# Four more attention weights split ahead of time, a narrower first query tile, and one block order swapped, in a two-layer decoder trunk

## The chip, the cores and the metric

The kernel runs on one core of a Trainium2 chip. The core has a matrix engine (TensorE: PE for the matrix products, PEld for the loads of the stationary operand that go with them), three engines for element-wise work (VectorE: DVE, ScalarE: ACT, GpSimd: POOL) and a queue engine (SyncE: SP) that issues the DMA transfers here. The metric is the time of one execution on the device in microseconds (us). Engines run side by side, each in its own fixed order of instructions, and wait for one another through semaphores.

## What is computed

Input `x` has 512 tokens of 1024 channels. The reference, cut to what matters here:

```python
for layer in range(2):
    h = rms_norm(x, mix_pre_g[layer])
    if layer == 0:
        m = pool_mixer(h, pool_w[0], pool_scale[0])          # causal averages, then 4 maps of 256x256
    else:
        q = h @ w_q                                          # 16 heads of 64
        o = stick_breaking_attention(q, k, v)                # key s < query t
        m = o @ w_o
    x = x + rms_norm(m, mix_post_g[layer])
    h = rms_norm(x, mlp_pre_g[layer])
    x = x + rms_norm(square(relu(h @ w_up[layer])) @ w_down[layer], mlp_post_g[layer])
    if layer == 0:
        k, v = split(rms_norm(x, kv_norm_g) @ w_kv)
```

In the attention, with `z = q k^T / 8`, a query's weight on key `s` is `sigmoid(z)` times the product of `1 - sigmoid(z)` over the keys between `s` and the query. Everything is float32.

## The kernel before

**Numbers in two parts.** A product in float32 is done as three products of a cheaper float32 form. Each operand is split into a high part (a rounding copy on ACT) and a low part (the difference, a subtraction on DVE); then high*high, high*low and low*high are added up in PSUM (`mm3`, and `up_block` for weights of which 128 columns stand in the array). A weight block of 128x1024 (512 KB) therefore costs a load, one ACT copy and one DVE subtraction before PE can use it. `weight` does this where the block is needed: it loads into a tile `raw`, copies the high part (L128) and subtracts the low part (L130).

**Weights kept in DRAM.** The layer-0 MLP also splits blocks for the attention in advance. `split_apart`, called once for each of the products of that MLP that `steps` lists, is a pipeline of four steps per block: load it into a free tile (`apart`, `spare` or `grow`); in the next call scale it on ACT if it carries a norm's gain (L139); in the next split it (L191 on ACT into `wx`, L192 on DVE back into its own tile); in the next store both parts to a DRAM tile `kept` (L172). Thirty blocks go this way: the value blocks `v`, the key and query blocks `k` and `q`, output blocks `o` 4 to 7, and two `up` blocks of the second MLP. When `make` later comes to such a block it issues two DMAs from `kept` (L202) and no engine has to split anything. Output blocks `o` 0 to 3 are not among the thirty and go through `weight`.

**Buffers.** Split weights live in three tiles tagged `w` and one tagged `wx`; up to four blocks are made ahead (`queue`, `made`, `ahead`). A load into such a tile waits until PE has finished with the block that was in it. `wx` is used by `split_apart` during the first MLP.

**The stages.** (1) Pooling mixer of layer 0, its order written out by hand (`MIX_ORDER`), with the first halves of four `up` blocks. (2) MLP of layer 0: 32 `up` blocks (`up_block`, 24 matmuls each) and, for 28 of them, the down projection as a Strassen-like scheme of seven products for each of five groups (`Seven`, L507; operands `a` and `w` are split by L242 on ACT and L243 on DVE, differences are built by POOL L462 and DVE L481). The last four blocks of the down projection, `dn`, are plain `mm3` (`contract`); their split tiles reuse buffers of the MLP, two of them the `apart` buffers. (3) Attention. (4) MLP of layer 1, as (2) without `split_apart`.

**The attention's order** is the table `ATT_ORDER`: V = `values` (value blocks of four heads, by key tile), K and P = projections of keys and queries of a pair of heads, S = `weights` (scores, sigmoids on ACT, the running product as a scan on DVE, L867, and one multiplication, L871), T = `transposed` (PE transposes, L885, split by L242 and L243), A = `mix_pair` (weights times values, L895), O and E = `out_proj` (output projection, `mm3`, by token tiles). So `V33` is the block of values 3 for key tile 3, and `O101` is the output projection with output blocks 2 and 3 for token tiles 0 and 1. The program text sets dependences and buffers; a scheduler then orders each engine's instructions by priority and estimated times, except where `manual_schedule` fixes an order.

Of the kernel before, what the change touches and what calls it, by code (L numbers as in the profile page):

```python
# [15 lines left out]
P = 128  # L16
# [36 lines left out]
ATT_ORDER = [  # L53
    (w[0], int(w[1]), [int(c) for c in w[2:]])
    for w in """V001 K0 V02 P0 V03 S0 P1 T0 V101 S1 A0 P2 T1 V123 A1 S2 P3 T2 O00123 A2 S3 P4 V201 T3 A3
    S4 P5 T4 V223 S5 A4 P6 V301 T5 S6 A5 P7 V32 T6 S7 O101 V33 A6 T7 A7 O12 O13 E2""".split()
]


# [6 lines left out]
def trunk(ctx, tc, x, consts, gcol, grow, pw, wup, wdn, wq, wk, wv, wo, out):  # L66
# [46 lines left out]
    behind, latest = {}, {}  # L113
# [29 lines left out]
    gate, queue, made, ahead, dn_pool, att_pool = [False], [], {}, 4, [None], [None]  # L143
# [21 lines left out]
    apart, kept, going = [], {}, []  # L165

    def split_apart(mp):
        if going and going[0][1] == 3:
            k, _, raw, hi, _ = going.pop(0)
            kept[k] = dram.tile([2, P, D], F32, tag=f"kept{len(kept)}", name=name("kept"))  # L170
            for n, t in enumerate((hi.bitcast(F32), raw)):
                latest["sp"] = nc.sync.dma_start(kept[k][n], t)  # L172
        if apart:
            k, src, scaled = apart.pop(0)
            n = len(apart) % 5
            if n < 3:
                raw = mp.tile([P, D], F32, tag="apart", bufs=3, name=name("apart"))
            else:
                raw = spare_tile() if n == 3 else work.tile([P, D], F32, tag="grow", name=name("apart"))

            with tc.issue_after(latest["sp"].ins) if "sp" in latest else nullcontext():
                nc.sync.dma_start(raw, src)
            going.append([k, 0, raw, None, scaled])
        for x in going:
            k, n, raw, hi, scaled = x
            if n == 1:
                if scaled is not None:
                    scaled(raw)
            elif n == 2:
                hi = x[3] = apart_hi[0][:, len(kept) % 2]  # L190
                nc.scalar.copy(hi, raw)  # L191
                nc.vector.tensor_tensor(out=raw, in0=raw, in1=hi.bitcast(F32), op=ALU.subtract)  # L192
            x[1] += 1
# [24 lines left out]
    for l in range(2):  # L218
        if l == 1:
            n = len(queue)  # L220
            for what, i, part in ATT_ORDER:
                if what == "V" and 0 in part:
                    for h in range(2):
                        want(("v", i, h), wv[i, h], gains(C_KV * KC + 4 * h, 4))
                elif what == "P":
                    want(("k", i), wk[i], gains(C_KV * KC, KC))
                    want(("q", i), wq[i], gains(C_MIX_PRE1 * KC, KC))
                elif what == "O" and 0 in part or what == "E":
                    for c in range(2 * i, 2 * i + (2 if what == "O" else 4)):
                        want(("o", c), wo[c])  # L230
            apart.extend(x for x in queue[n:] if x[0] not in [("o", c) for c in range(4)])
            apart.extend((("up", 1, j), wup[1, j], None) for j in range(2))

            queue[n - GRP : n + GRP] = queue[n : n + GRP] + queue[n - GRP : n]
        for j in range(NJ):
            want(("up", l, j), wup[l, j])
        for j in range(NJ - GRP, NJ):
            want(("dn", l, j), wdn[l, j])
# [279 lines left out]
    def mlp(l, mp, update):  # L518
# [4 lines left out]
        plain = 2 * sum(GROUPS)  # L523
        groups = [Seven(l, firsts[g], n, mp) for g, n in enumerate(GROUPS)]

        steps = [n for n in range(1, 34)] if l == 0 else []
        squares = []
        written = {None}

        def up(j, pu=None):  # L530
            if pu is None:
                pu = ps()
                up_block(pu, get(("up", l, j)), slice(0, S))
            if j < plain:
                g = max(g for g, f in enumerate(firsts) if f <= j)
                r = groups[g].part(j - firsts[g])
            else:
                r = mp.tile([P, S], F32, tag="rp", name=name("rp"))
            nc.scalar.activation(r, pu, ACT.Relu)
            nc.scalar.activation(r, r, ACT.Square)  # L540
            if j >= plain:
                if j < plain + 3:
                    if j == plain:
                        squares.append(mp.tile([P, 3, 2, S], F32R, tag="r", bufs=2, name=name("sq")))
                    a = squares[0][:, j - plain]
                else:
                    a = work.tile([P, 2, S], F32R, tag="spare", name=name("sq"))
                split(r, a[:, 0], a[:, 1])
                squares.append((a[:, 0], a[:, 1]))
            fill()  # L550
# [18 lines left out]
        for j, (pu, w) in enumerate(first):  # L569
            up_block(pu, w, slice(S // 2, S))  # L570
            up(j, pu)
        with tc.issue_after(latest["act"].ins), tc.issue_after(latest["dve"].ins):
            for i in range(2):
                groups[0].make(i)
        for g, group in enumerate(groups):
# [10 lines left out]
            for i in range(7):  # L586
# [12 lines left out]
                else:  # L599
# [4 lines left out]
                    elif i == 5:  # L604
                        piece = lambda tag, k, bufs=1: mp.tile([P, k, D], F32R, tag=tag, bufs=bufs, name=name("dn"))
                        w, e, x = piece("w1", 3), piece("e", 1), piece("w", 3, 2)
                        c, d = (piece("apart", 1, 3)[:, 0] for _ in range(2))
# [143 lines left out]
    with tc.tile_pool(name="att", bufs=1, reuse_waits="tile") as ap:  # L751
# [79 lines left out]
        for lo, n in SEG.values():  # L831
            c = min(n - P, 1)
# [9 lines left out]
        def weights(qk, a):  # L842

            q, k, kl, u = qk[0][a], qk[1][a], kls[a], us[a]
            w = ap.tile([P, NSEG], F32, tag="w", bufs=2, name=name("w"))
            for tiles, at in (((3,), 0), ((2,), 512), ((1, 0), 896)):
                pz = ps()
                o = 0  # L850
                for i in tiles:
                    n = max(256, (i + 1) * P)
                    nc.tensor.matmul(pz[:, o : o + n], q[:, TS[i]], k[:, :n], start=True, stop=False)  # L853
                    nc.tensor.matmul(  # L854
                        pz[:, o : o + n], q[:, TS[i]], kl[:, :n], start=False, stop=True
                    )
                    o += n
                o = 0
                for i in tiles:
                    n = SEG[i][1]  # L860
                    nc.scalar.activation(  # L861
                        u[:, at + o + 1 : at + o + n], pz[:, o + 1 : o + n], ACT.Sigmoid, scale=-0.125
                    )
                    o += n
                nc.scalar.activation(w[:, at : at + o], pz[:, :o], ACT.Sigmoid, scale=0.125)
            e = ap.tile([P, NSEG], F32, tag="e", name=name("e"))
            nc.vector.tensor_tensor_scan(  # L867
                out=e[:, ::-1], data0=u[:, 1:][:, ::-1], data1=begin[:, ::-1],
                initial=0.0, op0=ALU.mult, op1=ALU.max,
            )  # L870
            nc.vector.tensor_tensor(out=w, in0=w, in1=e, op=ALU.mult)  # L871
            return w
# [134 lines left out]
```

## Time and profile before

| | |
|---|---|
| three runs | 980.87, 982.71, 986.82 us; median 982.71 us |
| profiled execution | span 984.6 us from first to last instruction |
| PE | busy 959.1 us (97%), 4804 matmuls |
| PEld | 812.2 us (82%) |
| DVE | 715.6 us (73%) |
| ACT | 566.9 us (58%) |
| POOL | 138.5 us (14%) |
| DMA | 156.88 MB, 44.4% of the 16 engines' span |
| granted PE clock, mean | 0.990 |

The profiled execution's time is known only as its span; no time of its own around the span was recorded. The span lies 1.9 us above the median of the three runs and inside their range. In the profile a busy share of PE is not a measure of speed: matmuls overlap, and each is shown as longer than the distance to the next one. A full-rate matmul of 512 columns shows 0.39 us but the next starts 0.227 us later. What a wait costs is read from starts.

### The profile page before, as it was taken

The page shows a single profiled execution, that of the slowest core. Times are in us where ns is not written, and L with a number is a line of the kernel's source. Part 1 is how long each engine was busy: PE and PEld are TensorE (multiplying, and loading weights), DVE is VectorE, ACT ScalarE, POOL GpSimd, SP SyncE. Part 2 cuts the span into 40 slices and gives each one's busy share as a digit, 9 for nine tenths or more (in the row PEclk, how much of TensorE's full clock was granted, in tenths as well). Part 3 has the DMA queues.
Part 4 walks back from the last instruction along what each step waited for, and adds up shares of the span by engine and source line. Part 5 has one row for each costly group of instructions (what it writes and reads, how often), then busy time and mean ns, then how long its engine had stood idle before and what let it go on. Part 6 is the DMA issues. An engine that isn't in the chain of part 4 may idle for free.

```text
span 984.6 us, 12507 instructions
## 1 busy us (share of the span) xinstructions
PE 959.1 (97%) x4804; PEld 812.2 (82%) x4804; DVE 715.6 (73%) x772; ACT 566.9 (58%) x979; POOL 138.5 (14%) x107
## 2 busy tenths in 40 slices
PE   9799999999999999999999999989999999999997
PEld 6688888878788788999799987888888888888885
DVE  3647589897897986376667688775487785957856
ACT  4537888978695556465556573446454444444532
POOL 1102030130402204100000000302031210302103
PEclk9899999999999999999999999989999999999999
DMA  6153777959678690242352423243333314133012
GB/s 249 44 192 98 265 275 227 416 199 346 243 277 326 232 342 3 89 169 86 129 214 89 168 108 121 77 145 108 128 102 112 128 56 181 29 127 122 22 43 87
DMA packets 43550, 156.88 MB, mean 159 GB/s; under 512 B 4449, under 2 KB 4833, under 8 KB 43490
## 3 DMA queue, kind: packets, MB, share of 16 engines
q1 hardware_dynamic: 43490, 156.07, 44.4%
q8 instruction: 38, 0.62, 0.2%
q14 instruction: 22, 0.18, 0.1%
HBM read 122.50 MB, written 33.55 MB: 159 GB/s over the span
## 4 chain that ended last, share of the span: by engine, by line
PE 82%; DVE 8%; ACT 4%; issue 2%; DMA 2%; POOL 1%; POOLq 0%; DVEq 0%; ACTq 0%
PE ps L507 24%; PE ps L623 13%; PE ps L624 13%; PE ps L622 13%; PE ps L264 4%; PE ps L265 4%; PE ps L263 4%; DMA xn<-in_wdn 2%; PE ps L895 2%; DVE w L130 2%; PE ps L885 1%; DVE w L243 1%; PE ps L853 1%; PE ps L854 1%; ACT xn L246 1%
## 5 line engine op out<-in xcount | busy, mean ns | idle before, releaser
L507 PE MATMUL ps<-w,a 128*128 128x512 f32 x1176 | 278.4, 389 | 2.4 <-DVE a L243 2.4
L623 PE MATMUL ps<-xnl,w 128*128 128x512 f32 (+1 forms) x712 | 263.9, 371 | 1.9 <-DVE xnl L243 1.9
L624 PE MATMUL ps<-xnh,w 128*128 128x512 f32 (+1 forms) x712 | 263.5, 370 | 0.8 <-DVE w L130 0.8
L622 PE MATMUL ps<-xnh,w 128*128 128x512 f32 (+1 forms) x712 | 263.8, 372 | 0.4 <-ACT w L128 0.4
L507 PEld LDWEIGHTS ps<-w,a 128*128 128x128 f32 x1176 | 220.5, 188 | 49.4 <-DVE a L243 3.7
L623 PEld LDWEIGHTS ps<-xnl,w 128*128 128x128 f32 x712 | 136.3, 191 | 24.3 <-DVE xnl L243 2.5
L624 PEld LDWEIGHTS ps<-xnh,w 128*128 128x128 f32 x712 | 136.2, 191 | 23.2 <-DVE w L130 1.0
L622 PEld LDWEIGHTS ps<-xnh,w 128*128 128x128 f32 x712 | 135.8, 191 | 22.8 <-ACT w L128 0.6
L130 DVE TENSOR_TENSOR w<-raw,w 128x1024 fp32r<-128x1024 f32 x66 | 83.9, 1271 | 60.2 <-ACT w L128 60.2
L128 ACT CAST w<-raw 128x1024 fp32r<-128x1024 f32 x66 | 69.0, 1047 | 84.7 <-PE ps L624 79.0
L516 DVE TENSOR_TENSOR y<-ps,y 128x512 f32<-128x512 f32 x124 | 83.2, 683 | 34.9 <-PE ps L507 34.9
L242 ACT CAST a<-r 128x768 fp32r<-128x768 f32 (+1 forms) x60 | 47.6, 793 | 65.0 <-PE ps L507 39.4
L462 POOL TENSOR_TENSOR s<-r 128x768 f32<-128x768 f32 (+1 forms) x10 | 21.7, 2172 | 373.8 <-ACT r L540 331.2
L242 ACT CAST w<-e 128x1536 fp32r<-128x1536 f32 (+1 forms) x30 | 41.9, 1398 | 54.0 <-DVE e L481 44.7
L243 DVE TENSOR_TENSOR a<-r,a 128x768 fp32r<-128x768 f32 (+1 forms) x60 | 60.0, 1003 | 14.6 <-ACT a L242 14.5
L288 POOL TENSOR_TENSOR y<-y,grow 128x512 f32<-128x512 f32 x12 | 18.7, 1556 | 314.1 <-ACT xn L246 314.1
L243 DVE TENSOR_TENSOR w<-e,w 128x1536 fp32r<-128x1536 f32 (+1 forms) x30 | 58.3, 1943 | 4.5 <-ACT w L242 4.2
L462 POOL TENSOR_TENSOR r<-r 128x768 f32<-128x768 f32 (+1 forms) x20 | 48.7, 2437 | 64.5 <-DVE a L243 49.7
L867 DVE TENSOR_TENSOR_SCAN e<-u,begin 128x1280 f32<-128x1280 f32 x16 | 45.2, 2822 | 13.3 <-ACT u L861 13.0
L139 ACT ACTIVATE apart<-apart,gc 128x128 f32<-128x128 f32 (+1 forms) x132 | 42.8, 406 | 0.0
L246 ACT ACTIVATE xn<-y 128x512 f32<-128x512 f32 (+1 forms) x25 | 15.4, 616 | 41.8 <-DVE y L369 41.8
L243 DVE TENSOR_TENSOR w<-xn,w 128x1536 fp32r<-128x1536 f32 (+1 forms) x20 | 33.0, 1651 | 5.5 <-ACT w L242 5.5
(127 smaller groups left out, 1509.9 us busy)
## 6 DMA issues: line engine op xcount, KB each, us to landing
raw<-in_wup SPq DMA_DIRECT2D x62, 512.0 KB, 3.8
w<-kept SPq DMA_DIRECT2D x58, 512.0 KB, 4.2
kept<-wx SPq DMA_DIRECT2D x30, 512.0 KB, 5.2
w<-in_wdn SPq DMA_DIRECT2D x8, 1536.0 KB, 6.4
kept<-apart SPq DMA_DIRECT2D x24, 512.0 KB, 5.1
xn<-in_wdn SPq DMA_DIRECT2D x8, 1536.0 KB, 8.3
raw<-in_wdn SPq DMA_DIRECT2D x8, 512.0 KB, 4.3
apart<-in_wk SPq DMA_DIRECT2D x7, 512.0 KB, 8.8
```

Of the source, the lines that this page charges most:

```text
L128: nc.scalar.copy(hi, raw)
L130: nc.vector.tensor_tensor(out=lo, in0=raw, in1=hi.bitcast(F32), op=ALU.subtract)
L139: nc.scalar.mul(c, c, gc[:, lo + k : lo + k + 1])
L242: latest["act"] = nc.scalar.copy(hi, src)
L243: latest["dve"] = nc.vector.tensor_tensor(out=lo, in0=src, in1=hi.bitcast(F32), op=ALU.subtract)
L462: sub = lambda out, x, y, op=ALU.subtract: nc.gpsimd.tensor_tensor(out=out, in0=x, in1=y, op=op)
L507: nc.tensor.matmul(bank, a[:, x, q, TS[t]], w[:, z, q], start=start and q == 0 and k == 0, stop=q == self.n - 1 and k == 2, skip_group_che ...
L516: nc.vector.tensor_tensor(out=part, in0=bank, in1=part, op=ALU.add)
L622: nc.tensor.matmul(pu[:, cols], wh[:, k, :], xnh[:, k, cols], start=k == 0, stop=False)
L623: nc.tensor.matmul(pu[:, cols], wh[:, k, :], xnl[:, k, cols], start=False, stop=False)
L624: nc.tensor.matmul(pu[:, cols], wl[:, k, :], xnh[:, k, cols], start=False, stop=k == KC - 1)
L867: nc.vector.tensor_tensor_scan(out=e[:, ::-1], data0=u[:, 1:][:, ::-1], data1=begin[:, ::-1], initial=0.0, op0=ALU.mult, op1=ALU.max,)
```

## The change

Four edits. All eight output blocks now go through `split_apart`, 34 blocks instead of 30. `steps` now covers all 35 products of the first MLP, and two more calls stand ahead of the first product, after the second halves of `up` blocks 2 and 3. In the attention `V33` stands ahead of `O101`. Query tile 0 multiplies 128 keys and not 256; of its 256 columns only the first 128 had been read.

```diff
-    S4 P5 T4 V223 S5 A4 P6 V301 T5 S6 A5 P7 V32 T6 S7 O101 V33 A6 T7 A7 O12 O13 E2""".split()
+    S4 P5 T4 V223 S5 A4 P6 V301 T5 S6 A5 P7 V32 T6 S7 V33 O101 A6 T7 A7 O12 O13 E2""".split()
...
-            apart.extend(x for x in queue[n:] if x[0] not in [("o", c) for c in range(4)])
+            apart.extend(queue[n:])
...
-        steps = [n for n in range(1, 34)] if l == 0 else []
+        steps = [n for n in range(35)] if l == 0 else []
...
             up_block(pu, w, slice(S // 2, S))
             up(j, pu)
+            if l == 0 and j >= 2:
+                with tc.issue_after(latest["act"].ins), tc.issue_after(latest["dve"].ins):
+                    split_apart(mp)
...
-                    n = max(256, (i + 1) * P)
+                    n = (i + 1) * P
```

The insertion shifts lines from 572 on by three: the scan L867 of the profile is L870 in the changed kernel, L885 is L888, L895 is L898.

**Start of the first MLP, ACT.** The rows are ACT's, at the fourth and fifth `up` block; `r` are activations, `a` is an operand of the first two products, `w` are split `up` weights. Before:

```order
L539 ACTIVATE r_536<-ps_466 128x512
L128 CAST w_610<-raw_611 128x1024
L540 ACTIVATE r_536<-r_536 128x512
L539 ACTIVATE r_536<-ps_500 128x512
L242 CAST a_673<-r_536 128x512
```

The same place of the changed kernel:

```order
L139 ACTIVATE apart_674<-apart_674,gc 128x256 x4
L540 ACTIVATE r_536<-r_536 128x512
L539 ACTIVATE r_536<-ps_466 128x512
L128 CAST w_610<-raw_611 128x1024
L539 ACTIVATE r_536<-ps_500 128x512
L191 CAST wx_537<-spare_646 128x1024
L540 ACTIVATE r_536<-r_536 128x512 x2
L242 CAST a_681<-r_536 128x512
```

Scaling and splitting of the first value blocks now stand ahead of the first product's operand `a`.

**End of the first MLP, DVE.** `a_2873`, `w_2876` before and `a_2896`, `w_2899` now are the operands of the last product, `dn` the split blocks of the plain down projection. Before:

```order
L192 TENSOR_TENSOR apart_2739<-apart_2739,wx_537 128x1024
L130 TENSOR_TENSOR dn_2908<-raw_2939,dn_2907 128x1024
L516 TENSOR_TENSOR y_532<-ps_2576,y_532 128x512
L243 TENSOR_TENSOR sq_2836<-rp_2833,sq_2836 128x512
L516 TENSOR_TENSOR y_533<-ps_2577,y_533 128x512
L243 TENSOR_TENSOR a_2873<-r_2101,a_2873 128x768
L516 TENSOR_TENSOR y_530<-ps_2879,y_530 128x512
L243 TENSOR_TENSOR w_2876<-xn_80,w_2876 128x1536
```

Now:

```order
L192 TENSOR_TENSOR apart_2760<-apart_2760,wx_537 128x1024
L516 TENSOR_TENSOR y_532<-ps_2597,y_532 128x512
L243 TENSOR_TENSOR sq_2859<-rp_2856,sq_2859 128x512
L516 TENSOR_TENSOR y_533<-ps_2598,y_533 128x512
L243 TENSOR_TENSOR a_2896<-r_2130,a_2896 128x768
L130 TENSOR_TENSOR dn_2933<-raw_2967,dn_2932 128x1024
L516 TENSOR_TENSOR y_530<-ps_2902,y_530 128x512
L243 TENSOR_TENSOR w_2899<-xn_80,w_2899 128x1536
L192 TENSOR_TENSOR apart_2827<-apart_2827,wx_537 128x1024
```

The low part of the third `dn` block has moved four instructions back, to just ahead of the last product's `w`, and one more block is split behind that `w`. `dn_2933` takes the buffer of `apart_2760`, so it waits for the store of that tile.

On PE the same place now reads as follows (`ps_2978` is the first bank of the plain down projection):

```order
L263 MATMUL ps_2978<-dn_2932,sq_2654 128x512
L507 MATMUL ps_2597<-w_2899,a_2896 128x512
L507 MATMUL ps_2598<-w_2899,a_2896 128x512
L264 MATMUL ps_2978<-dn_2933,sq_2654 128x512
L265 MATMUL ps_2978<-dn_2932,sq_2654 128x512
```

Seven matmuls of the plain down projection and two of the last product stand ahead of the first use of `dn_2933`, and eleven more behind it before the rest of the last product; before, all of the first 18 were laid around the two.

**The attention's last scans, DVE.** `e` are the scans of the last pair of heads, `w_5010` before is output block 3, `v` the values of `V33`, `al` the low part of transposed weights. Before:

```order
L867 SCALAR_TENSOR_TENSOR e_5145<-u_3160,begin 128x1280
L871 TENSOR_TENSOR w_5126<-w_5126,e_5145 128x1280
L867 SCALAR_TENSOR_TENSOR e_5167<-u_3161,begin 128x1280
L871 TENSOR_TENSOR w_5148<-w_5148,e_5167 128x1280
L130 TENSOR_TENSOR w_5010<-raw_5011,w_5010 128x1024
L770 TENSOR_TENSOR v_4797<-ps_5212,v_4797 128x4x64
L243 TENSOR_TENSOR al_5121<-ps_5119,ah_5120 128x256
```

Now:

```order
L870 SCALAR_TENSOR_TENSOR e_5165<-u_3188,begin 128x1280
L874 TENSOR_TENSOR w_5146<-w_5146,e_5165 128x1280
L773 TENSOR_TENSOR v_4821<-ps_5193,v_4821 128x4x64
L870 SCALAR_TENSOR_TENSOR e_5187<-u_3189,begin 128x1280
L874 TENSOR_TENSOR w_5168<-w_5168,e_5187 128x1280
L243 TENSOR_TENSOR al_5141<-ps_5139,ah_5140 128x256
```

The split of output block 3 is gone, and the values of `V33` stand ahead of the second scan. On PE the 24 matmuls of `V33` now come ahead of the 12 with output block 2, where they came behind them, and the first four matmuls with output block 3 stand after the first transposes of T7 and just ahead of the matmul that needs this `al`.

## The prediction

> **What bounds the kernel now.** I read first the busy shares, then the chain of waits, then a table by stage; the first line is the chain that ended last, by engine, the second the first MLP.
>
> ```profile
> PE 82%; DVE 8%; ACT 4%; issue 2%; DMA 2%; POOL 1%; POOLq 0%; DVEq 0%; ACTq 0%
> 64.00:386.00 322.00, 319.54 (x1459) 265.33 (x1458) 265.41 (x253) 234.39 (x393) 59.21 (x28) 1.00 0.71 255
> ```
>
> The second line holds start and end, length, busy time and count of PE, PEld, DVE, ACT and POOL, the PE clock, the DMA share, GB/s. PE is busy for 319.5 of 322 us, and the chain of the whole program runs through PE for 82%. So work taken from DVE or ACT is worth nothing except where PE stands for it. Of the first MLP's 322 us DVE works 265 and ACT 234: the splits that the change adds there find room on the average, and can hurt only at one place. What is left to win is PE's stalls next to an edited line.
>
> **Two splits in O00123 go.** PE first, then DVE:
>
> ```profile
> 480.68 0.47 PE L263 MATMUL ps<-w,ohl 128*128 128x512 f32 x1 [0.52 <-DVE kl L809]
> 481.46 0.40 PE L263 MATMUL ps<-w,ohl 128*128 128x512 f32 x1
> 482.06 0.50 PE L264 MATMUL ps<-w,ohl 128*128 128x512 f32 x1 [0.21 <-DVE w L130]
> 482.40 0.40 PE L265 MATMUL ps<-w,ohl 128*128 128x512 f32 x1
> 483.51 0.50 PE L263 MATMUL ps<-w,ohl 128*128 128x512 f32 x1 [0.70 <-DVE al L243]
> ...
> 480.79 1.23 DVE L130 TENSOR_TENSOR w<-raw,w 128x1024 fp32r<-128x1024 f32 x1 [0.25 <-ACT w L128]
> ```
>
> A full-rate matmul of 512 columns takes 0.23 us from start to start (twelve of them in 2.79 between 589.00 and 591.79, rows further on). So 481.46 to 482.06 loses 0.37, 482.40 to 483.51 loses 0.88, and the first wait is 0.52: 1.8 in all. The last is for `al`, subtractions that DVE starts only after the split of 480.79. That split (1.23) and the one of the other block in front of it go, so DVE comes 1.2 us or more earlier to each of these, more than any of the waits. **Term: -1.8**, bounds 0 (a late block from `kept` takes their place) and -1.8.
>
> **The split in O101 goes, V33 moves ahead.** The window behind the stall, then PE, DVE and the queue:
>
> ```profile
> 599.70:603.20 3.50, 3.50 (x9) 2.80 (x10) 2.54 (x5) 0.00 (x0) 0.00 (x0) 0.51 0.49 150
> ...
> 589.00 0.39 PE L263 MATMUL ps<-w,ohl 128*128 128x512 f32 x1
> 591.79 0.28 PE L263 MATMUL ps<-w,xnh 128*128 128x256 f32 x1
> 594.65 0.39 PE L895 MATMUL ps<-ah,v 128*128 128x512 f32 x1
> 596.53 1.10 PE L263 MATMUL ps<-w,ohl 128*128 128x512 f32 x4
> 597.46 0.28 PE L895 MATMUL ps<-ah,v 128*128 128x256 f32 x1
> 599.67 0.78 PE L264 MATMUL ps<-w,ohl 128*128 128x512 f32 x1 [1.93 <-DVE w L130]
> 603.20 0.22 PE L895 MATMUL ps<-ah,v 128*128 128x128 f32 x1
> 603.95 0.23 PE L895 MATMUL ps<-ah,v 128*128 128x128 f32 x1
> ...
> 594.03 2.83 DVE L867 TENSOR_TENSOR_SCAN e<-u,begin 128x1280 f32<-128x1280 f32 x1
> 596.99 1.49 DVE L871 TENSOR_TENSOR w<-w,e 128x1280 f32<-128x1280 f32 x1
> 598.40 1.22 DVE L130 TENSOR_TENSOR w<-raw,w 128x1024 fp32r<-128x1024 f32 x1
> 599.53 0.42 DVE L770 TENSOR_TENSOR v<-ps,v 128x256 fp32r<-128x256 f32 x1
> 599.87 0.41 DVE L243 TENSOR_TENSOR al<-ps,ah 128x256 fp32r<-128x256 f32 x1
> ...
> w<-kept SPq DMA_DIRECT2D x58, 512.0 KB, 4.2
> kept<-apart SPq DMA_DIRECT2D x24, 512.0 KB, 5.1
> ```
>
> This is the largest stall. PE starts a matmul of 256 columns (0.12) at 597.46 and the next at 599.67: 2.1 us lost, for a split that stands on DVE behind the scan of 594.03 and its multiplication. Then eight matmuls take 603.20 - 599.67 = 3.53 where 8 x 0.23 = 1.84 would do, at a clock of 0.51: 1.7 more. The place costs 3.8.
>
> What is late next? DVE still has the scan, and the values of V33 now ahead of it. Those take 0.34 (599.53 to 599.87), so the second multiplication starts at about 597.33, ends 1.41 later (596.99 to 598.40 is its distance) at 598.74, and `al` behind it is done at 599.15. PE reaches the matmul that reads this `al` so: from 589.00, V33 2.86 (591.79 to 594.65), twelve products with block 2 2.79 (589.00 to 591.79), ten with transposed weights 1.88 (594.65 to 596.53), a pair of 128 with four transposes and one of 256 0.7 (603.20 to 603.95 holds such a set), four with block 3 0.93 (596.53 to 597.46): 598.2. A stall of 1.0 us for `al` takes the place of 2.1 for the split. Does the clock fall again? Stalls of that length stand at the starts of groups of the first MLP:
>
> ```profile
> 205.80 2.58 PE L507 MATMUL ps<-w,a 128*128 128x512 f32 x10 [0.74 <-DVE a L243]
> 206.00:209.00 3.00, 3.00 (x14) 2.44 (x14) 3.00 (x3) 3.00 (x9) 2.30 (x1) 1.00 0.58 236
> ```
>
> After it the clock reads 1.00 for the next 3 us, so I keep no loss of clock. **Term: -2.8** (2.1 + 1.7 - 1.0); bounds -3.8 (no new stall) and 0 (the new wait as long as the old, clock lost again). One more condition is thin: block 3 now comes by two loads from `kept`, into a buffer that V33 sets free at about 591.9; at the median of 4.2, behind one other pair, they land by 596.1 to 597.3, and PE asks at 597.2.
>
> [...]
>
> **Query tile 0 with 128 keys.** Sixteen heads, two matmuls each: 32 go from 256 to 128 columns. A 256 pair, and a 128 pair that the trace has elsewhere, each followed by a 512:
>
> ```profile
> 441.41 0.23 PE L895 MATMUL ps<-ah,v 128*128 128x128 f32 x1
> 441.58 0.45 PE L895 MATMUL ps<-ah,v 128*128 128x512 f32 x1
> 441.87 0.40 PE L895 MATMUL ps<-al,v 128*128 128x512 f32 x1
> ...
> 587.48 0.28 PE L853 MATMUL ps<-k,q 128*128 128x256 f32 x1
> 587.72 0.40 PE L853 MATMUL ps<-k,q 128*128 128x512 f32 x1
> 587.95 0.39 PE L854 MATMUL ps<-kl,q 128*128 128x512 f32 x1
> ```
>
> To the start of the second 512 it is 0.46 with the short pair and 0.47 with the long one: the short pair takes 0.17 instead of 0.24, and the matmul behind it 0.29 instead of 0.23. **Term: -0.2** (16 x 0.015); bounds 0 and -1.1 (16 x 0.07, if nothing is given back). [...]
>
> **Start of the first MLP.** ACT gets two calls of `split_apart` before the first product.
>
> ```profile
> 80.61 1.06 ACT L128 CAST w<-raw 128x1024 fp32r<-128x1024 f32 x1 [2.00 <-DMA raw<-in_wup]
> 82.58 0.60 ACT L242 CAST a<-r 128x512 fp32r<-128x512 f32 x1
> 84.31 1.07 PE L507 MATMUL ps<-w,a 128*128 128x512 f32 x4
> 97.35 1.71 ACT L139 ACTIVATE apart<-apart,gc 128x256 f32<-128x256 f32 x4
> 105.50 1.05 ACT L191 CAST wx<-apart 128x1024 fp32r<-128x1024 f32 x1
> ```
>
> Two scalings and one split, 1.71 + 1.71 + 1.05 = 4.5, come ahead of the copy of 82.58, which ends by 83.1 and which PE takes up at 84.31. ACT stands idle for 2.00 here, until the load at 80.61, and more of the first scaling lies ahead of that. If 3.0 of the 4.5 are covered so, the copy ends at 84.6, and PE waits **0.4**, with DVE's low part right behind; bounds 0 (all covered but what the 1.2 in hand takes) and +1.5 (2.0 covered: 85.6 with a little of the rest overlapped).
>
> **End of the first MLP.** The split of the third `dn` block waits for a store of the tile that it overwrites.
>
> ```profile
> 359.77 0.57 SPq L172 DMA_DIRECT2D kept<-apart  x1
> 363.79 0.39 PE L263 MATMUL ps<-dn,sq 128*128 128x512 f32 x1
> 180.06 10.19 DMA xn<-in_wdn
> ```
>
> The tile's low part is made by DVE at about 357.3 as before; a store then lands 5.1 later by the median, at 362.4, or 10.2 later, at 367.5, if it fares as the slow load of the last row. PE asks for the block seven plain matmuls and two of the last product behind 363.79 (9 x 0.23), at 365.8. I take a landing of 365.2, between the two, as the stage's DMA share is 0.71; the split (1.22) is done at 366.4: **+0.6**, bounds 0 and +2.9 (368.7). Meanwhile DVE stands, and behind it an output sum (L516) and the last product's `w`, one and a half times as wide as the split; PE has eleven more plain matmuls (2.5) before it needs that, which hides it.
>
> **What costs nothing.** Four more blocks are 4 loads that stood elsewhere, 8 stores and 8 reads instead of raw loads: 16 transfers or 8 MB more, against 156.88 MB, most of them in a stage whose DMA share is 0.71; a full stage of 322 us can take 25 GB/s on top of 255. Their splits, 4 x (1.05 ACT + 1.22 DVE), lie in the MLP's slack of 88 us on ACT and 57 on DVE; without that cover they would be 9 us, the far end of what this edit could cost.
>
> **Sum.** -1.8 - 2.8 - 0.2 + 0.4 + 0.6 = -3.8 on the profiled span of 984.6, which gives 980.8. That span lies 1.9 above the median 982.71; taken from the median, **979.0**. A measurement tells about 1%, 9.8 us, from nothing: faster begins at 972.9, slower at 992.5.
>
> **Rivals.** *All of it goes:* `al` is in time, the ends of the first MLP show nothing, 128 keys save fully: -1.8 - 3.8 - 1.1 = -6.7, **976**. For it: both starts and ends have slack of their own; against: the scan of 2.83 still stands ahead of `al`. Chance 0.13. *The stall in O101 is only renamed:* with 1.0 of stall and the clock lost again it is -2.8 + 1.7 = -1.1, whole sum -2.1; with block 3 late from `kept` it is 0, whole sum -1.0: **981 to 982**. For it: the half clock stands behind a gap of 2.1, and I have no row that says where between 1.0 and 2.1 it begins. Chance 0.22. *Slower, by the store at the end of the first MLP:* the queue hands it over only where it handed over the store of before (359.77, behind loads from `kept` that wait for their own buffers), and it takes 10.2: it lands at 370.0, the split is done at 371.2, PE stands from 365.8 on for 5.4, and a gap of that length loses the clock as in O101, 1.7 more. In place of +0.6 that is +7.1, whole sum +2.7: **985.4**. From a landing at 367.3 on (a stall of 2.7 and the clock) it outweighs all the rest. For it: DVE's wait stands in front of everything else there; against: the median of 5.1. Chance 0.1. *It does not do what it says:* the four blocks are split early, but come from `kept` too late each time, so that PE waits for a load where it waited for DVE; the added terms alone count, +1.0 - 0.2: 983.5. Chance 0.05. The forecast has 0.5.
>
> **Range.** The renamed stall and most of the slow store lie above, the full gain below: **974.5 to 984.0**. Beyond the 1% bounds: slower 0.04 (that store still later, or the 9 us of splits uncovered), faster 0.06 (only if more goes than every stall named here), within 0.9.
>
> **What would show it.** No wait for L130 by PE around 480; no clock under 0.9 behind 600; a wait of about 1 us for L243 `al` near 596; 128 pairs with a longer matmul behind them; PE's wait for `dn` near 366 under 1 us; 165 MB moved. Wrong if the first MLP grows by over 3 us, or if the last attention stage still shows 0.51.

## The result, and the profile after

The changed kernel takes **980.19 us** (median of 20 runs), the kernel before, run beside it, 985.26 us (median of 20). The ratio is **0.9958, 95% interval 0.9940 to 0.9976**: 4.1 us less, 2.4 to 5.9 by the interval. (It is not the quotient of the two medians, which is 0.9949 or 5.1 us; both lie in the interval.) A second comparison on another occasion gave 0.9952 (0.9929 to 0.9975). The forecast was 979.0, or -3.8 us, and no change by the 1% bound. The profiled execution took 982.03 us, with a span of 980.1; single executions of either kernel lie up to 7 us from the median, and the table of stages below shows which stages vary.

The chain that ended last, by engine, the first MLP and the attention (columns as before the change), and the traffic:

```profile
PE 73%; DVE 12%; DMA 7%; ACT 4%; issue 4%; POOL 1%; SPq 0%; POOLq 0%; DVEq 0%; ACTq 0%
...
64.00:386.00 322.00, 317.63 (x1448) 262.69 (x1449) 270.45 (x254) 234.07 (x388) 60.38 (x26) 1.00 0.76 275
386.00:638.00 252.00, 251.48 (x1494) 223.09 (x1493) 173.77 (x213) 140.72 (x318) 18.32 (x34) 1.00 0.36 130
...
DMA packets 45854, 165.27 MB, mean 169 GB/s; under 512 B 4705, under 2 KB 5089, under 8 KB 45794
```

PE's busy time in the first MLP has fallen (319.54 to 317.63 in the same 322 us), DVE's has risen by 5.0. The chain now runs through DMA for 7% where it was 2%, and through DVE for 12% where it was 8%. This is no sign of the change by itself: one of the kernels below, whose first MLP is that of before, has 5% and 11% (the swap alone). 165 MB move instead of 157.

**Around 480**, PE, then DVE. The three waits are gone, and so are the two splits in DVE's row:

```profile
484.07 0.48 PE L263 MATMUL ps<-w,ohl 128*128 128x512 f32 x1
484.38 0.39 PE L264 MATMUL ps<-w,ohl 128*128 128x512 f32 x1
484.61 0.40 PE L265 MATMUL ps<-w,ohl 128*128 128x512 f32 x1
...
482.85 0.69 DVE L812 TENSOR_TENSOR kl<-ps,k 64x512 fp32r<-64x512 f32 x1 [1.24 <-ACT k L811]
483.57 0.69 DVE L821 TENSOR_TENSOR q<-ps,q 64x512 fp32r<-64x512 f32 x1
484.29 1.62 DVE L243 TENSOR_TENSOR al<-ps,ah 128x512 fp32r<-128x512 f32 x3
```

**Around 600**, PE, then DVE. Two short waits stand where one of 2.1 us and a lost clock stood:

```profile
598.87 0.36 PE L898 MATMUL ps<-ah,v 128*128 128x256 f32 x1
599.39 1.20 PE L263 MATMUL ps<-w,ohl 128*128 128x512 f32 x4 [0.16 <-DMA w<-kept]
600.71 0.39 PE L898 MATMUL ps<-al,v 128*128 128x256 f32 x1
600.93 0.23 PE L898 MATMUL ps<-ah,v 128*128 128x128 f32 x1
...
595.65 0.42 DVE L773 TENSOR_TENSOR v<-ps,v 128x256 fp32r<-128x256 f32 x1
595.98 2.82 DVE L870 TENSOR_TENSOR_SCAN e<-u,begin 128x1280 f32<-128x1280 f32 x1
598.83 1.49 DVE L874 TENSOR_TENSOR w<-w,e 128x1280 f32<-128x1280 f32 x1
600.24 0.42 DVE L243 TENSOR_TENSOR al<-ps,ah 128x256 fp32r<-128x256 f32 x1
```

From 598.87 a matmul of 256 columns should be followed after 0.12 (24 of them took 2.86 in the kernel before, 591.79 to 594.65) and is followed after 0.52: 0.4 lost, for block 3 coming from `kept`. The four matmuls from 599.39 should take 0.93 (596.53 to 597.46 before) and PE goes on after 1.32 (600.71): another 0.3 to 0.4, for `al`, which DVE has ready at 600.66.

**The first MLP**: a group's first product in the middle, and the end of the stage (the store on SP, DVE, PE).

```profile
193.51 2.52 DVE L481 TENSOR_TENSOR e<-xn,w 128x1536 f32<-128x1536 f32 x1 [3.47 <-DMA xn<-in_wdn]
205.08 0.96 PE L507 MATMUL ps<-w,a 128*128 128x512 f32 x3 [1.00 <-DVE w L243]
209.94 3.47 PE L507 MATMUL ps<-w,a 128*128 128x512 f32 x14 [1.17 <-DVE a L243]
...
360.69 0.32 SPq L172 DMA_DIRECT2D kept<-apart  x1
368.59 1.23 DVE L130 TENSOR_TENSOR dn<-raw,dn 128x1024 fp32r<-128x1024 f32 x1 [1.24 <-DMA kept<-apart]
368.70 0.61 PE L507 MATMUL ps<-w,a 128*128 128x512 f32 x2
369.87 0.50 PE L264 MATMUL ps<-dn,sq 128*128 128x512 f32 x1 [0.55 <-DVE dn L130]
```

The store goes out at 360.69 and DVE waits for it until 368.59, 7.9 later; PE loses 0.7 (368.70 to 369.87 is 1.17 for two matmuls of 0.23). That is the wait that the prediction described. In the middle of the stage stand two waits of 1.0 and 1.2 us behind a load of `xn` for which DVE stood 3.47; before, one of 0.74 stood there (205.80).

**By stage.** PE's matmuls, 4804 of them in every kernel, are counted from the first one on, and each cell is the distance in us between the starts of two of them in the trace. The order within a stage differs, its count does not. Rows with * are experiments described below.

| kernel | 400 to 1800: first MLP | 1800 to 2400: with O00123 | 2400 to 2800 | 2800 to 3200: with O101 | 3200 to 3400: E2, start of MLP 2 | 3400 to 4800 |
|---|---|---|---|---|---|---|
| before | 315.92 | 99.66 | 67.73 | 73.63 | 32.49 | 311.38 |
| changed | 318.86 | 97.39 | 67.65 | 70.25 | 29.97 | 311.38 |
| changed, second profile * | 317.19 | 97.39 | 67.65 | 70.25 | 31.36 | 311.38 |
| first MLP alone * | 316.05 | 99.64 | 67.73 | 73.62 | 31.09 | 311.38 |
| attention alone * | 315.33 | 97.38 | 67.65 | 70.25 | 29.98 | 311.38 |
| changed without the swap * | 315.60 | 97.38 | 67.65 | 73.41 | 32.36 | 311.38 |
| 128 keys alone * | 314.51 | 99.59 | 67.66 | 72.04 | 32.41 | 311.38 |
| swap alone * | 319.27 | 99.66 | 67.74 | 70.98 | 32.30 | 311.38 |
| 32 blocks * | 319.88 | 97.39 | 67.65 | 70.95 | 31.31 | 311.38 |
| pairs exchanged * | 319.76 | 97.38 | 67.65 | 70.25 | 31.46 | 311.38 |
| changed, half the stores * | 314.01 | 97.39 | 67.65 | 70.25 | 31.31 | 311.38 |
| before, half the stores * | 313.25 | 99.65 | 67.73 | 72.09 | 31.34 | 311.38 |
| no blocks of MLP 2 * | 315.20 | 97.38 | 67.65 | 70.27 | 31.97 | 311.38 |

Read down a column: the last one shows that a stage without waits repeats to 0.01 us, the second and third take two values each, within 0.1, according to one edit. The first, the fourth and the fifth also vary between executions of the same code. The mixer ahead of matmul 400, which the change does not touch, lies between 70 and 76 us in these profiles. The second profile of the changed kernel was taken to see what is chance in the first: its first MLP, 317.19, lies between the two expected answers (318 to 319 if all of the growth belonged to the change, 315.5 to 317 if most of it did not), and 31.36 in the fifth column says that the 29.97 of the first profile was no effect of the change.

### The profile page after: what moved, and what is told of

Its sections match the earlier page's. It is cut to its first block, busy times and chain, and to the rows that moved or that the text cites. A ratio compares the mean times of both kernels' runs of the same rounds, so it can differ in the third digit from the quotient of the medians.

```text
span 980.1 us, 12542 instructions
## 1 busy us (share of the span) xinstructions
PE 957.6 (98%) x4804; PEld 810.4 (83%) x4804; DVE 718.3 (73%) x772; ACT 565.7 (58%) x979; POOL 143.0 (15%) x107
## 4 chain that ended last, share of the span: by engine, by line
PE 73%; DVE 12%; DMA 7%; ACT 4%; issue 4%; POOL 1%; SPq 0%; POOLq 0%; DVEq 0%; ACTq 0%
PE ps L507 19%; PE ps L627 11%; PE ps L626 11%; PE ps L625 11%; PE ps L264 4%; PE ps L265 4%; PE ps L263 4%; DMA xn<-in_wdn 3%; PE ps L898 2%; DVE w L130 2%; DVE w L243 2%; PE ps L888 2%; DVE apart L192 1%; DVE e L481 1%; DVE y L516 1%
## 5 line engine op out<-in xcount | busy, mean ns | idle before, releaser
L627 PEld LDWEIGHTS ps<-xnh,w 128*128 128x128 f32 x712 | 134.8, 189 | 23.2 <-DVE w L130 1.0
L625 PEld LDWEIGHTS ps<-xnh,w 128*128 128x128 f32 x712 | 134.4, 189 | 22.9 <-ACT w L128 0.6
L128 ACT CAST w<-raw 128x1024 fp32r<-128x1024 f32 x62 | 64.9, 1048 | 70.1 <-PE ps L627 66.1
L243 DVE TENSOR_TENSOR a<-r,a 128x768 fp32r<-128x768 f32 (+1 forms) x60 | 62.4, 1043 | 12.4 <-ACT a L242 12.3
L462 POOL TENSOR_TENSOR r<-r 128x768 f32<-128x768 f32 (+1 forms) x20 | 53.8, 2691 | 70.0 <-DVE a L243 69.2
L870 DVE TENSOR_TENSOR_SCAN e<-u,begin 128x1280 f32<-128x1280 f32 x16 | 45.1, 2822 | 13.2 <-ACT u L864 13.0
L139 ACT ACTIVATE apart<-apart,gc 128x128 f32<-128x128 f32 (+1 forms) x116 | 39.0, 417 | 0.0
L192 DVE TENSOR_TENSOR apart<-apart,wx 128x1024 f32<-128x1024 f32 x27 | 37.8, 1401 | 1.1 <-ACT wx L191 1.1
```

Source lines behind the costliest of these rows:

```text
L243: latest["dve"] = nc.vector.tensor_tensor(out=lo, in0=src, in1=hi.bitcast(F32), op=ALU.subtract)
L462: sub = lambda out, x, y, op=ALU.subtract: nc.gpsimd.tensor_tensor(out=out, in0=x, in1=y, op=op)
L625: nc.tensor.matmul(pu[:, cols], wh[:, k, :], xnh[:, k, cols], start=k == 0, stop=False)
L627: nc.tensor.matmul(pu[:, cols], wl[:, k, :], xnh[:, k, cols], start=False, stop=k == KC - 1)
L870: nc.vector.tensor_tensor_scan(out=e[:, ::-1], data0=u[:, 1:][:, ::-1], data1=begin[:, ::-1], initial=0.0, op0=ALU.mult, op1=ALU.max,)
```

## The experiments

**The first MLP alone, and the attention alone.** The first keeps the changed MLP and undoes the attention; the second, in the kernel before, does the reverse. Of each edit the line on the output blocks is shown; the order of `V33` and the keys of query tile 0 are set to match:

```diff
-        if k in kept:
+        if k in kept and k not in [("o", c) for c in range(4)]:
```
```diff
+        if k in [("o", c) for c in range(4)]:
+            kept[k] = kept["o", k[1] + 4]
         if k in kept:
```

> The first MLP of the changed kernel (34 blocks split ahead, two early calls), with the attention of before: output blocks 0 to 3 are loaded raw and split again in the attention, V33 behind O101, 256 keys for query tile 0. Theory A (the prediction's sum): only its two added waits count, +0.4 and +0.6, so +1.0 on before, ratio 1.001. Theory B (the two profiles: matmul 400 to 1800 of the program grew by 2.95 us, of which 1.6 stand around 203 to 209 where the operand of a Strassen product came late): the extra transfers cost about 3 us, ratio 1.003. Theory C: the growth in that profile was chance; the first MLP then comes out between 0 and +1 longer and shows no wait over 1.1 us around 205. The stalls of 1.8 near 480 and of 2.1 near 600 must be back.

Measured: ratio 1.0014 (0.9997 to 1.0031), +1.4 us. Its first MLP takes 316.05, against 315.92 before and 318.86 in the first profile of the changed kernel; it has the wait for `dn` (0.6), none at the start, and no wait over 0.9 in the middle. So this run does not show the 2.95 us by which the two first profiles differ to belong to the change; the interval, up to 3.1 us, does not exclude it either (theory B). The stalls near 480 and 600 are back to 0.02 us (99.64, 73.62).

> The first MLP of before (30 blocks), with the attention of the changed kernel: output blocks 0 to 3 are read from the kept blocks 4 to 7, so the weights of those four blocks are the wrong ones, and nothing but the values differs. V33 ahead of O101, 128 keys. Prediction's sum: -1.8 - 2.8 - 0.2 = -4.8, ratio 0.995. From the two profiles: -2.3 around 480 and -3.4 around 600, so -5.7, ratio 0.994; if the clock that did not fall behind the stall near 648 belongs to the change, -8, ratio 0.992. If that clock is chance, it falls in some profiles and not in others, whatever the kernel.

Measured: 0.9932 (0.9908 to 0.9956), -6.7 us, within an interval that holds -5.7 and -4.8. The two halves add up to -5.3, beside -4.1 for the whole; the intervals overlap widely.

**The changed kernel without the swap, and the swap alone.** The one line of the attention's order, in the changed kernel and in the kernel before:

```diff
-    ... T6 S7 V33 O101 A6 ...
+    ... T6 S7 O101 V33 A6 ...
```

> The changed kernel with V33 behind O101 again. Theory A: the swap hides the wait for the low part of the last transposed weights: without it PE comes to that matmul about 1 us earlier with nothing to do in between and waits about 2 us instead of 0.3, and may lose the clock as before (1.7): +1.3 to +3.4 on the changed kernel, ratio to before 0.997 to 0.999. Theory B: the gain near 600 comes from the split that is gone alone, and the swap is worth nothing: same as the changed kernel, ratio 0.996.

Measured: 0.9997 (0.9981 to 1.0014): 4 us worse than the changed kernel, all of the gain; 3.2 of it stand in this stage (73.41 against 70.25). PE and DVE of that kernel:

```profile
593.15 0.28 PE L898 MATMUL ps<-ah,v 128*128 128x256 f32 x1
595.50 0.33 PE L898 MATMUL ps<-ah,v 128*128 128x128 f32 x1 [2.08 <-DVE v L773]
...
590.66 2.83 DVE L870 TENSOR_TENSOR_SCAN e<-u,begin 128x1280 f32<-128x1280 f32 x1
593.62 1.49 DVE L874 TENSOR_TENSOR w<-w,e 128x1280 f32<-128x1280 f32 x1
595.03 0.42 DVE L773 TENSOR_TENSOR v<-ps,v 128x256 fp32r<-128x256 f32 x1
```

The split is gone and PE waits as long as with it, and loses the clock behind it as well: now for the values of V33, which stand behind the scan and its multiplication. Theory A had the size (2 us and the clock) and the wrong name: it is `v` that is late first, not `al`.

> Before with V33 ahead of O101 and nothing else; all four output blocks are still split in the attention. Theory A (both parts are needed at this place, as the run without the swap suggests): the split still stands behind a scan, PE waits as long as before, ratio 1.000. Theory B (the swap alone does it): in the new order the split of block 3 stands behind the second scan but ahead of its multiplication, so it is done near 598.2 on the clock of the first profile, where PE asks at 597.6; a wait of 0.6 us takes the place of 2.1, and the gap is too short to lose the clock. Then -1.5 to -3.2, ratio 0.997 to 0.9985; the stalls near 480 stay.

Measured: 0.9969 (0.9951 to 0.9987). Theory B. The split of block 3 stands between the second scan and its multiplication, and PE waits 0.4 (0.55 from the start of a 256 to the next start, which should be 0.12):

```profile
596.25 0.28 PE L895 MATMUL ps<-ah,v 128*128 128x256 f32 x1
596.80 0.50 PE L264 MATMUL ps<-w,ohl 128*128 128x512 f32 x1 [0.27 <-DVE w L130]
...
595.54 1.20 DVE L130 TENSOR_TENSOR w<-raw,w 128x1024 fp32r<-128x1024 f32 x1
596.99 1.48 DVE L871 TENSOR_TENSOR w<-w,e 128x1280 f32<-128x1280 f32 x1
```

So the swap alone takes the stage from 73.63 to 70.98; the split of block 3 gone on top of it is worth 0.7 (70.25), and without the swap 0.2 (73.41). Of the 2.65 of the swap, 1.6 is the clock, which the kernel before does not lose each time (next experiment).

**128 keys alone.** The edit of that one line in the kernel before.

> Before with 128 keys for query tile 0 and nothing else. Prediction: -0.2, that is a ratio of 1.000; by the far bound -1.1, ratio 0.999. In the trace a pair of 128 should stand 0.12 to 0.17 apart from the next matmul where a pair of 256 took 0.24, with the next matmul of 512 late by what was saved.

Measured: 0.9992 (0.9975 to 1.0009), which cannot tell -0.2 from nothing; the table can: -0.07 in each of two stages (99.59 and 67.66). In the changed kernel the row reads

```profile
589.29 0.22 PE L856 MATMUL ps<-k,q 128*128 128x128 f32 x1
589.35 0.27 PE L857 MATMUL ps<-kl,q 128*128 128x128 f32 x1
589.45 0.45 PE L856 MATMUL ps<-k,q 128*128 128x512 f32 x1
589.74 0.39 PE L857 MATMUL ps<-kl,q 128*128 128x512 f32 x1
```

A pair is the product with the high and the one with the low part of the keys: 0.16 for the short pair, 0.29 for the matmul behind it, 0.45 together where the long pair made 0.47. The more telling row of this run is another one. PE has the stall of 2.1 us for the split as before, and the window behind it reads

```profile
596.70:598.50 1.80, 1.68 (x7) 1.42 (x8) 1.65 (x5) 0.00 (x0) 0.00 (x0) 1.00 0.43 64
```

a clock of 1.00, where it was 0.51 in the kernel before. The same gap is followed by half clock in one execution and by full clock in another, and the traces show what goes with it. In each of the thirteen profiles the granted clock changed only at points that lie whole multiples of 3.41 us apart; in the kernel before these are, among others, 599.72, 603.13 (599.72 + 3.41), 650.92 and 657.74 (14 and 16 times 3.413 behind 603.13). Cut along these points, into stretches, the kernel before and this run read (length, then PE busy, then the other columns as above):

```profile
596.30:599.72 3.42, 1.49 (x9) 1.03 (x7) 3.29 (x4) 0.14 (x1) 0.00 (x0) 1.00 0.27 109
599.72:603.13 3.41, 3.41 (x8) 2.76 (x9) 2.45 (x5) 0.00 (x0) 0.00 (x0) 0.50 0.50 154
...
595.16:598.58 3.42, 1.76 (x8) 1.45 (x9) 3.27 (x6) 0.00 (x0) 0.00 (x0) 1.00 0.24 36
598.58:602.00 3.42, 3.42 (x30) 3.24 (x28) 3.36 (x6) 2.77 (x6) 0.00 (x0) 1.00 0.47 145
```

PE's idle time in the table runs from the shown end of one matmul to the start of the next.

| kernel | PE idle | of it in one stretch, and in the next | clock of the 3.41 us that follow |
|---|---|---|---|
| before | 597.74 to 599.67 | 1.93 | 0.50 |
| first MLP alone | 596.69 to 598.61 | 1.93 | 0.50 |
| changed without the swap | 593.43 to 595.50 | 2.08 | 0.50 |
| 128 keys alone | 594.87 to 596.82 | 0.29, 1.66 | 1.00 |
| before, half the stores | 595.84 to 597.78 | 1.31, 0.62 | 1.00 |

From 60 to 960 us the thirteen profiles hold over 3400 stretches at full clock. All 13 in which PE stood idle for 1.93 us or more were followed by half clock, none with 1.66 or less was, and of the five between 1.71 and 1.89 three were. Where the program lies against these points differs from one profile to the next: the gap begins 1.98 us ahead of one in the kernel before and 0.29 in this run. So the five rows do not show that an edit sets whether a gap of 2 us costs the clock.

**32 blocks.** Output blocks 2 and 3 are split in the attention again, with the swap kept, and the two early calls dropped (`apart.extend(x for x in queue[n:] if x[0] not in [("o", 2), ("o", 3)])`).

> The changed kernel with 32 blocks split ahead (output blocks 2 and 3 go through the attention's own split again) and without the two early calls. If the swap alone settles the place near 600, this keeps the gain of 2.3 near 480 and that of 1.5 to 3.2 near 600, and pays only for two more blocks in the first MLP (the wait for the store, 0.4 to 0.7): ratio 0.994 to 0.997, as good as the changed kernel or 1 us better. If the split of block 3 has to go, the stall of 2 us is back there: ratio 0.998.

Measured: 0.9970 (0.9949 to 0.9992). The stage with O101 is that of the swap alone (70.95). Its first MLP shows 319.88, the longest of all, with two blocks added instead of four: how long that stage is does not follow from the number of blocks. In this profile and in that of the swap alone (319.27) some 1.7 of it (an estimate, half of 3.41) is a clock of 0.50 for 3.41 us, behind a stall of 1.4 us at the start of a group (330.17 and 325.24).

**Half the stores.** Only the high part of each block is stored, and read in place of both, in the changed kernel and in the kernel before:

```diff
-            for n, t in enumerate((hi.bitcast(F32), raw)):
+            for n, t in enumerate((hi.bitcast(F32),)):
...
-                latest["sp"] = nc.sync.dma_start(t.bitcast(F32), kept[k][n])
+                latest["sp"] = nc.sync.dma_start(t.bitcast(F32), kept[k][0])
```

> The changed kernel with only the high part of each block stored, and read twice: 34 stores of 512 KB fewer, low parts wrong. Theory A (the first MLP pays for transfers): loads of xn land in 5 to 7 us instead of 7.6 and more, matmul 400 to 1800 takes 315 us instead of 316 to 319, and the wait for dn's buffer is gone, so that all in all it is 1 to 3 us faster than the changed kernel: ratio to before 0.993 to 0.995. Theory B (the first MLP pays for DVE's and ACT's work, or for nothing but the wait at its end): 0.5 us faster at most, ratio 0.9955.

> Before with only the high part of each of the 30 blocks stored, and read twice (30 stores of 512 KB fewer, low parts wrong). Theory A (the stalls at the starts of the groups of the first MLP, 1.4 to 4.6 us in the profiles so far whatever the number of split blocks, come from transfers that queue up): matmul 400 to 1800 falls from 314.5 to 319 us to about 314, ratio 0.996 to 0.999. Theory B (they come from DVE's and ACT's load, and the half stores were faster in the changed kernel by chance or by the wait for dn's buffer alone): no change against before, which has no such wait, ratio 1.000.

Measured: changed kernel with half the stores 0.9934 (0.9910 to 0.9957) to before; kernel before with half the stores 0.9973 (0.9958 to 0.9988). Their first MLPs are the two shortest of the table, 314.01 and 313.25. Of the kernel before with half the stores, the first MLP and the start of the group that waited 0.74 at 205.80, now without a wait (206.17 to 206.40 is 0.23); then a line of the DMA issues, before and with half the stores (from issue to landing last):

```profile
64.00:386.00 322.00, 321.57 (x1479) 267.93 (x1478) 266.05 (x257) 236.74 (x395) 58.63 (x29) 1.00 0.59 206
206.17 0.39 PE L624 MATMUL ps<-xnh,w 128*128 128x512 f32 x1
206.40 3.34 PE L507 MATMUL ps<-w,a 128*128 128x512 f32 x14
...
kept<-wx SPq DMA_DIRECT2D x30, 512.0 KB, 5.2
kept<-wx SPq DMA_DIRECT2D x30, 512.0 KB, 4.0
```

DVE's and ACT's work is the same (266.05 and 236.74), only the DMA share falls, from 0.71 to 0.59, and PE's waits of over 0.6 us at the starts of the groups go in both. In this stage the 1.5 MB loads of `xn` land after 7.9 us by the median where they took 9.7, and DVE stands for them 4.5 us in all where it stood 10.7; with the changed kernel these are 8.2 for 9.9 and 6.5 for 12.6. Theory A for the kernel before, whose interval leaves out 1.000. For the changed kernel the ratio alone cannot tell A from B (the interval holds 0.9955, and the changed kernel run beside it had 0.9952), and the loads did not come down to 5 to 7 us; its profile speaks for A. The change's own wait for the tile's store goes there as well.

**No blocks of the second MLP.** The two `up` blocks and the early calls dropped: 32 blocks in 35 calls.

> The changed kernel with its eight output blocks split ahead, but without the two blocks of the second MLP and without the two early calls: 32 blocks in 35 calls. The second MLP splits those two blocks itself, where PE stands for 3.4 us near 648 anyway. If the added transfers and the early calls are what the first MLP pays for, it is 0.5 to 1.5 us faster than the changed kernel, ratio 0.994 to 0.996. If the second MLP's start depends on those blocks, stage 3200 to 3400 grows from 30.0 to 32.5 by 1 us or more and the ratio is 0.997.

Measured: 0.9970 (0.9951 to 0.9990), not better than the changed kernel. Its first MLP is 315.20; in the stage behind E2 PE now stands twice (2.3 and 1.9 us). The stage takes 31.97 in all, within what it takes in the other profiles, so that this is not shown to be the price.

**Pairs exchanged.** `dn_pool`'s third and fourth pair change places, so that the third `dn` block does not wait for the store.

> The changed kernel with the buffers of the third and fourth block of the plain down projection exchanged: the third takes the tile of a finished operand w, the fourth those of the split blocks. Theory A: the wait for the store at the end of the first MLP (0.4 to 0.7 us of PE in four profiles) goes, 0.5 us faster than the changed kernel, ratio 0.9950. Theory B: the low part of the last product's w, which PE now needs earlier, takes its place: ratio 0.9955, with a wait for L243 w of 0.5 us at the end of the first MLP.

Measured: 0.9985 (0.9962 to 1.0008), an interval that leaves out both forecasts. The second of the two waits is the one that theory B named; the first, for ACT's copy of `dn`, neither had:

```profile
363.23 0.50 PE L263 MATMUL ps<-dn,sq 128*128 128x512 f32 x1 [1.08 <-ACT dn L128]
364.86 1.43 PE L507 MATMUL ps<-w,a 128*128 128x512 f32 x5 [1.12 <-DVE w L243]
```

The wait of 0.55 has become two of 1.1. None of the versions that compute the same is shown to beat the changed kernel.

## Why the prediction was right

**The sum**: forecast -3.8, measured -4.1 (-2.4 to -5.9). The median that goes with -3.8 is 978.9 and not 979.0. That the two come so close is in part luck: the attention's three edited stages gave 5.7 in the profiles where 4.8 was forecast, the first MLP alone +1.4 where it was +1.0, and the intervals are far too wide to tell such parts.

**Around 480**: forecast -1.8, measured 2.27 in each of the eight profiles without these splits, or 2.2 without the 128 keys' share. The mechanism was right, the size short by 0.4 and beyond the term's far bound, which was -1.8 too: the first wait was taken as the 0.52 of idle time that its row names, where starts give 0.7, and behind each of the three waits the next matmul came after 0.31 to 0.34 instead of 0.23 (482.06 to 482.40), which the sum left out.

**Around 600**: forecast -2.8, measured -3.4 against the profile of before (73.63 to 70.25, of which 0.03 is the keys') and -1.8 against the two that kept their clock there (72.04, 72.09). The new wait was named rightly, `al` behind the second scan, and the thin condition too: block 3's load is 0.4 late. Together they are 0.7 and not 1.0, and the clock stayed, in line with the stretches above: 0.7 is far below the 1.71 us of idle time of the least stretch that lost it. The 1.7 for the clock was in the sum only because the profile of before had lost it; two of five profiles with such a gap had not. What the prediction had wrong is the credit. It gave the place to the split that goes and booked the swap as 0.34 of delay; the runs show that the split's going is worth 0.2 without the swap, and that the swap alone takes 2.65 off that place, of which 1.6 is the clock that is not lost behind the shorter wait. The sum of this place came out near because the prediction followed both edits together through the new order.

**128 keys**: forecast -0.2, measured -0.07 in each of two stages and about -0.03 in the third, -0.17. The short pair gives back to the next matmul what it saves, as the rows of other places had said. The starts of the short pair, 589.29 and 589.35, are 0.06 apart, and the time is lost two matmuls further on.

**Start and end of the first MLP**: forecast +0.4 and +0.6. The wait at the start is 0.55 in the first profile of the changed kernel and under 0.2 in its second, in the first MLP alone and in the kernel without the swap; the wait at the end is there in all four, 0.7, 0.6, 0.6 and 0.4. The store landed 7.9 after its issue at 360.69, which came as soon as DVE had made the low part (360.65); the prediction too had 7.9 (357.3 to 365.2), but as a choice between 5.1 and 10.2, so that this match is luck. The rival by that store did not come: the queue did not hold the store back.

**What costs nothing**: this is where the prediction was thin. It looked at the mean DMA share of the stage (0.71) and at the slack of DVE and ACT. The half stores show that transfers do cost PE time there, 2.7 us in the kernel before alone: the stage's share is a mean, and the waits stand where a 1.5 MB load lands late, and with half the stores it lands 1.8 us earlier. What the change's own transfers in this stage (8 stores more, and 4 loads that stood in the attention) add is not settled: the stage grew by 2.9 in the first profile, just under the 3 us that the prediction had named as a sign of being wrong, and by 1.3 in the second; the first MLP alone gives +1.4 (-0.3 to +3.1), and the profiles with the old first MLP (314.5 to 319.3) overlap those with the new one (315.6 to 319.8).

**Not from the change, and not in the sum**: the start of the second MLP is 2.5 us shorter in the changed kernel's first profile. Behind a stall of 3.4 us that stands in both, the clock is 0.50 before and 1.00 after (end of the stall and on):

```profile
651.50:653.50 2.00, 1.81 (x9) 1.84 (x10) 0.77 (x3) 0.59 (x1) 0.00 (x0) 0.50 0.00 0
650.00:652.00 2.00, 1.82 (x15) 1.65 (x16) 1.23 (x2) 1.12 (x3) 0.00 (x0) 1.00 0.00 0
```

The second profile of the same changed kernel has 31.36 there, and the thirteen profiles lie between 29.97 and 32.49. Again it goes with where the stall falls: PE is idle there for about 3.3 us in twelve of them. In the kernel before 2.50 of it lies in one stretch and 0.78 in the next, and the clock stays at half for two stretches (6.83 us); in the first profile of the changed kernel it is 1.89 and 1.39, and the clock stays full; in its second, 0.20 and 3.08, and it is half for one stretch. From the two first profiles alone, 2.5 us of gain here and 2.95 of loss in the first MLP would have been put down to the change.

## What to carry to other kernels

When an instruction that PE waits for is taken out of an in-order engine's queue, look at what else of PE's stands behind the same long instruction; here a scan of 2.8 us held three things, and moving one of them ahead was worth more than removing another (2.65 us, of which 1.6 is the clock, against 0.2). A transfer that only feeds a later stage can cost a stage that PE fills (here 2.7 us, with the stores of the kernel before): its mean DMA share says little, the landing times of the largest loads (here 9.7 us with all stores, 7.9 with half) say more. And before a difference between two profiles is put down to an edit, compare stage by stage over several profiles: a stage that repeats to 0.01 us can be trusted, one that moves by 4 us between runs of like code cannot. Look for a clock that was lost in one and not in the other first.

## What the runs showed of the hardware that I had not expected

A gap on PE of 2.1 to 2.2 us was followed by half clock for 3.41 us in three profiles and by full clock in two, which is 1.6 us on the stage (73.6 against 72.1). What went with it was how much of PE's idle time fell into one of the stretches of 3.41 us between the points at which the clock changed in these profiles: after 1.93 us and more it was half each time, after 1.66 and less never. Between 60 and 960 us of the thirteen profiles, a stretch at half clock with 0.51 us of idle time or less was followed by full clock, and one with 0.78 to 1.20 by another at half; so the gap of 3.4 us cost between 0 and 2.5 us. Stores of 512 KB that nobody waits for took 2.7 us out of 984 in the kernel before (ratio 0.9973, 0.9958 to 0.9988, when 30 of them were left out), through loads that land later beside them (9.7 against 7.9 us).
